# A product moved between its neighbours in units of seven products: two-layer decoder trunk on one Trainium2 core

## The chip, the cores and the metric

The kernel runs on one core of one Trainium2 chip. The metric is the device time of one launch in microseconds (us). Most executions of a kernel agree within 0.3%. The kernel before took 1681.06 us, the median of three runs (1681.12, 1681.06, 1673.86).

## What is computed

The reference is a decoder trunk over 2048 positions of width 1024, in float32: one layer that mixes positions by a short convolution, one layer of attention without softmax, and three norms. Cut to what matters:

```python
h = rmsnorm(x, norm_a)                                   # layer 0
b, c, xin, g = split(h @ w_in, 4)                        # w_in: 1024 x 4096
y = b * causal_conv3(c * xin)
x = x + (y * silu(g)) @ w_out                            # w_out: 1024 x 1024
k, v = split(rmsnorm(x, norm_kv) @ w_kv, 2)              # 8 heads of 64
q, g = split(rmsnorm(x, norm_b) @ w_in_b, 2)             # layer 1
o = stick_breaking_attention(q, k, v)                    # causal, per head
x = x + (o * silu(g)) @ w_out_b
return rmsnorm(x, norm_f)
```

## The kernel before, in words

Activations lie transposed: 128 features on the partitions, positions along the free side, in four chunks of 512 columns (CH=512). Every float32 operand of a matmul is held as a high and a low part in a reduced format, and a product of two operands takes three matmuls (high x high, high x low, low x high) for each 128 rows of the contraction.

**Units of seven products.** The big projections are not done block by block. For two chunks and two blocks of 128 output features, four 128x512 results are made by seven block products in place of eight (the method of Strassen and Winograd). Each product contracts over 512 features: 4 steps (Q=4) of 3 matmuls, so 12 matmuls of 128x512. There are 44 such units: 28 in the first layer's input projection (parts m02 to m07 for chunks 0 and 1, m20 to m27 for chunks 2 and 3; names with B and C), 8 in its output projection (po00 to po03 and po20 to po23; names with o0 to o3, followed by the chunk 0 or 2), and 8 in the projections after it for chunks 0 and 1 (kq0 to kq3, vg0 to vg3).

Three functions make a unit. `fast_operands` (L731) makes seven right operands per pair of chunks (for chunks 0 and 1 of the first projection another function does it, which the change leaves alone), named b11, t1, t2, b22, b21, t3, t4, each in four k-tiles: it loads tiles, takes differences on VectorE (DVE), copies the high part on ScalarE (ACT) and subtracts to get the low part on VectorE, or on GpSimd (POOL) for b21 and t3 of the out units and of the kq and vg units (`late`, L739). `fast_weights` (L771) loads the seven left operands (a11, s1, s2, s4, a12, s3, a22), 512 KB each, through SyncE's queue (SP) in the order of `NAMES`, into a ring of eight tiles. `fast_unit` (L816) issues the products:

- Bank `a` (tag lin, two buffers; traced as fa) is the shared accumulator. It takes a11·b11, s2·t2, s3·t3 and a22·t4 one after the other, and after each of them an engine reads the partial sum: c11 (keep f1), c12 (keep f2), p5, and the last result. The next product into the bank must wait until that read is done.
- Bank `d` (tag z, three buffers; fd) takes s1·t1 (read into p5, keep f5), then s4·b22 (added to c12).
- Bank `e` (tag wt, two buffers; fe) takes a12·b21 alone (added to c11).

In the units of the first projection, and in kq and vg, a keep is a copy by ScalarE. In the out units it is an addition on VectorE of the residual tile (traced as x), which SyncE has loaded from the input; p5 and the sums with d and e are additions on VectorE in every unit.

**The order.** The body isn't emitted as written. A recorder (`Recorder`, L205 to L353) collects all operations of all parts; the table PLAN gives each part a start and an end, an operation's key is its place in its part between them, and `Recorder.order` puts the operations on the engines in turn: the one that can start first by built-in costs, and of equals the one with the lower key. So the order in which a unit is written moves the keys of its operations, and with them operations of all engines in this and in neighbouring parts. Every operation is issued at one line and shows as L353 in the profile; tiles tell them apart. In the trace fa_o is bank a of an out unit, whl_s_o and whl_a_o its left operands, op_t and op_b right operands, xb_kq and op_b_kq the tiles of which the operands of kq and vg are made.

## Time and profile before

| | value |
|---|---|
| profiled execution, own time | 1683.09 us |
| its span, first to last instruction | 1680.9 us |
| median of the three timed runs | 1681.06 us |
| TensorE (PE) busy | 1623.6 us, 97% |
| VectorE (DVE) busy | 1345.1 us, 80% |
| ScalarE (ACT) busy | 787.7 us, 47% |
| GpSimd (POOL) busy | 524.6 us, 31% |
| mean granted TensorE clock | 0.992 |

A row of a timeline gives start, duration, engine, line, operation, output and inputs, tile size, the number of instructions in the row, and in brackets the engine's idle time before it with what ended it. A row of windows gives the stretch, its length, and the busy time of PE, of PE's weight loads (PEld), DVE, ACT and POOL, then the granted TensorE clock, the share of the DMA engines and GB/s. A row of waits gives who waited for whom, the sum in us, how often, and the longest.

On TensorE the last matmuls of the out units of chunks 0 and 1 lie near 726 us of the span, those of chunks 2 and 3 end near 817 us; the kq and vg units follow until about 980 us, with the first of attention among them.

### The profile page before, as it was taken

Reading aid. Unit: us, or ns where it says so; the run is one execution under the profiler, and the core shown is the slowest. Engines: PE = TensorE matmul, PEld = TensorE weight load, DVE = VectorE, ACT = ScalarE, POOL = GpSimd, SP = SyncE. Lnnn points to the kernel's source line nnn. Section 1 sums busy time; section 2 is a strip of 40 time slices with the busy share of each in tenths; the row PEclk is TensorE's granted clock in tenths of the full one; section 3 lists DMA queues with packets and bytes.
Section 4 is the critical chain, followed back from the end, with each engine's and each line's share of the span. In section 5 each row is a group of like instructions: output and inputs, shape, how many; then the busy total and the mean of one; then the engine's idle time right before and its main releaser. Section 6 shows DMA issues by size and latency. Waiting matters only on the chain.

```text
span 1680.9 us, 23871 instructions
## 1 busy us (share of the span) xinstructions
PE 1623.6 (97%) x7828; PEld 1339.8 (80%) x7828; DVE 1345.1 (80%) x1944; ACT 787.7 (47%) x1483; POOL 524.6 (31%) x708
## 2 busy tenths in 40 slices
PE   6999999999999999998999999999999999999896
PEld 5878888888888887877778877887888888888775
DVE  6998788885436349798898788968999988999895
ACT  5444444432213125432544455645556656667452
POOL 5340000000000002357643142333333444556534
PEclk9999999999999999999999999999999999999997
DMA  9458889884473569999677899998756788779744
GB/s 275 163 182 307 296 303 306 278 304 145 147 213 97 192 208 314 365 353 345 213 240 248 288 368 299 357 278 244 222 182 184 229 261 283 247 237 282 228 158 140
DMA packets 226251, 419.48 MB, mean 250 GB/s; under 512 B 21072, under 2 KB 94800, under 8 KB 226128
## 3 DMA queue, kind: packets, MB, share of 16 engines
q1 hardware_dynamic: 194656, 358.15, 63.3%
q10 hardware_dynamic: 31312, 59.79, 12.4%
q8 instruction: 62, 1.02, 0.3%
q14 instruction: 61, 0.50, 0.1%
q0 software_dynamic: 160, 0.02, 0.0%
HBM read 265.06 MB, written 152.83 MB: 249 GB/s over the span
## 4 chain that ended last, share of the span: by engine, by line
PE 75%; DMA 7%; DVE 6%; issue 2%; ACT 2%; POOL 1%; SPq 0%; ACTq 0%; POOLq 0%; DVEq 0%
PE fa_B L353 9%; PE fa_C L353 9%; PE av L353 7%; PE z L353 6%; PE wt L353 6%; PE fd_B L353 5%; PE fd_C L353 4%; PE pob L353 4%; PE fa_o L353 3%; PE fe_C L353 2%; PE fe_B L353 2%; PE pg L353 2%; PE pq L353 2%; PE fa_kq L353 2%; PE pv L353 2%; PE pk L353 2%
## 5 line engine op out<-in xcount | busy, mean ns | idle before, releaser
L353 DVE TENSOR_TENSOR_SCAN R<-R,cy,ones 128x512 f32<-128x512 f32 x192 | 246.3, 1311 | 2.4 <-ACT R L353 2.1
L353 ACT CAST wth<-wt 128x512 fp32r<-128x512 f32 (+2 forms) x320 | 154.4, 526 | 178.9 <-PE wt L353 141.3
L353 DVE TENSOR_TENSOR wtl<-wt,wth 128x512 fp32r<-128x512 f32 (+2 forms) x320 | 180.6, 599 | 37.6 <-ACT wth L353 34.6
L353 PE MATMUL z<-kt,q 128*128 128x512 f32 (+2 forms) x640 | 179.1, 379 | 4.4 <-DMA q<-q_d 2.0
L353 ACT ACTIVATE R<-z 128x512 f32<-128x512 f32 (+2 forms) x320 | 158.9, 545 | 39.8 <-PE z L353 34.5
L353 PE MATMUL wt<-ident,R 128*128 128x128 f32 x1088 | 168.4, 273 | 0.1
L353 POOL COPY halo<-p 128x2 f32<-128x2 f32 x32 | 15.7, 490 | 482.2 <-DVE p L353 482.2
L353 PEld LDWEIGHTS wt<-ident,R 128*128 128x128 f32 x1088 | 133.4, 141 | 21.1 <-DVE R L353 0.7
L353 POOL COPY cy<-R 128x1 f32<-128x1 f32 x192 | 100.5, 526 | 135.8 <-DVE R L353 117.6
L353 PEld LDWEIGHTS z<-kt,q 128*128 128x128 f32 x640 | 111.4, 190 | 23.2 <-ACT R L353 4.5
L353 PE MATMUL av<-wth,vv 128*128 128x512 f32 (+1 forms) x320 | 119.5, 374 | 9.9 <-ACT wth L353 9.1
L353 PE MATMUL av<-wtl,vv 128*128 128x512 f32 (+1 forms) x320 | 122.7, 387 | 0.5 <-DVE wtl L353 0.4
L353 DVE TENSOR_TENSOR_SCAN R<-R,ones 128x256 f32<-128x256 f32 (+3 forms) x128 | 103.8, 838 | 8.8 <-POOL R L353 7.8
L353 POOL TENSOR_SCALAR_AFFINE_SELECT R<-R 128x128 f32<-128x128 f32 x128 | 68.1, 545 | 117.6 <-ACT R L353 116.4
L353 PE MATMUL pob<-og,whl_ob 128*128 128x512 f32 x360 | 102.8, 404 | 0.6 <-DVE x L353 0.4
L353 POOL TENSOR_TENSOR acc_x<-acc_x,sq_x 128x512 f32<-128x512 f32 x52 | 73.8, 1424 | 63.0 <-ACT sq_x L353 61.2
L353 PE MATMUL fa_C<-op_t,whl_s_C 128*128 128x512 f32 x336 | 85.2, 391 | 0.7 <-DVE op_t L353 0.7
L353 PE MATMUL fa_B<-op_t,whl_s_B 128*128 128x512 f32 x336 | 84.9, 390 | 0.0
L353 PEld LDWEIGHTS av<-wth,vv 128*128 128x128 f32 x320 | 60.4, 189 | 26.9 <-ACT wth L353 12.8
L353 PEld LDWEIGHTS fa_C<-op_t,whl_s_C 128*128 128x128 f32 x336 | 62.9, 188 | 14.7 <-DVE op_t L353 1.1
L353 PEld LDWEIGHTS pob<-og,whl_ob 128*128 128x128 f32 x360 | 64.6, 189 | 12.5 <-DVE x L353 0.8
L353 PEld LDWEIGHTS fa_B<-op_t,whl_s_B 128*128 128x128 f32 x336 | 63.0, 188 | 12.9
(581 smaller groups left out, 3779.4 us busy)
## 6 DMA issues: line engine op xcount, KB each, us to landing
kt<-k_d ACTq DMA_DIRECT2D x80, 256.0 KB, 4.6
vv<-v_d ACTq DMA_DIRECT2D x80, 256.0 KB, 4.7
q<-q_d ACTq DMA_DIRECT2D x64, 256.0 KB, 6.3
sw_s_C<-whl_s_C SPq DMA_DIRECT2D x24, 512.0 KB, 3.7
sw_s_B<-whl_s_B SPq DMA_DIRECT2D x24, 512.0 KB, 4.4
whl_s_C<-sw_s_C SPq DMA_DIRECT2D x24, 512.0 KB, 4.3
whl_s_B<-sw_s_B SPq DMA_DIRECT2D x24, 512.0 KB, 4.3
whl_ob<-sw_ob SPq DMA_DIRECT2D x24, 512.0 KB, 5.2
```

Of the source, the lines that this page charges most:

```text
L353: getattr(o.engine.engine, o.name)(*map(real, o.args), **{k: real(v) for k, v in o.kw.items()})
```

## The change

Three edits go together. In `fast_operands` the four t3 operands are made before the loop that loads and makes the four of b21, where the two took turns before. `NAMES` lists s3 ahead of a12, so left operands are loaded in that order. In `fast_unit` s3·t3 and the addition to p5 come right behind s4·b22, and a12·b21 with the addition to c11 comes between s3·t3 and a22·t4. The same seven products are made of the same operands.

```diff
@@ fast_operands
         d = []
         for k in range(Q):
+            operand(key, "t3", k, b[k], late)
+        for k in range(Q):
             d.append(raw("b21", 1, k + Q))
             operand(key, "b21", k, d[k], late)
-            operand(key, "t3", k, b[k], late)
@@
-    NAMES = ("a11", "s1", "s2", "s4", "a12", "s3", "a22")
+    NAMES = ("a11", "s1", "s2", "s4", "s3", "a12", "a22")
@@ fast_unit
         product(d, "s4", "b22", False, True)
         nc.vector.tensor_add(c12, c12, d)
+        product(a, "s3", "t3", False, False)
+        nc.vector.tensor_add(p5, p5, a)
         product(e, "a12", "b21", True, True)
         nc.vector.tensor_add(c11, c11, e)
-        product(a, "s3", "t3", False, False)
-        nc.vector.tensor_add(p5, p5, a)
         product(a, "a22", "t4", False, True)
         return ((c12, p5), (c11, a))
```

What the recorder makes of it is seen in the order of instructions on the engines. From about 1080 us of the trace of before to its end, the order on every engine is the same in both kernels. Three places follow; a row is output, left of the arrow, and inputs, and x3 stands for three matmuls alike.

**TensorE, end of unit o1 of chunk 2.** Before, bank a of o2 (fa_o2_2) follows on the last product of o1, then comes the first product of o3:

```order
L353 MATMUL fa_o1_2_6483<-op0_t4_('o', 2)_3_6686,whl_a22_o1_2_6566 128x512
L353 MATMUL fa_o1_2_6483<-op1_t4_('o', 2)_3_6711,whl_a22_o1_2_6566 128x512
L353 MATMUL fa_o1_2_6483<-op0_t4_('o', 2)_3_6686,whl_a22_o1_2_6566 128x512
L353 MATMUL fa_o2_2_6762<-op_t2_('o', 2)_0_6355,whl_s2_o2_2_6760 128x512 x3
L353 MATMUL fa_o2_2_6762<-op_t2_('o', 2)_1_6384,whl_s2_o2_2_6760 128x512 x3
L353 MATMUL fa_o2_2_6762<-op_t2_('o', 2)_2_6415,whl_s2_o2_2_6760 128x512 x3
L353 MATMUL fa_o2_2_6762<-op_t2_('o', 2)_3_6420,whl_s2_o2_2_6760 128x512 x3
L353 MATMUL fd_o2_2_6782<-op_b22_('o', 2)_0_6241,whl_s4_o2_2_6767 128x512 x3
L353 MATMUL fd_o2_2_6782<-op_b22_('o', 2)_1_6248,whl_s4_o2_2_6767 128x512 x3
L353 MATMUL fd_o2_2_6782<-op_b22_('o', 2)_2_6256,whl_s4_o2_2_6767 128x512 x3
L353 MATMUL fd_o2_2_6782<-op_b22_('o', 2)_3_6263,whl_s4_o2_2_6767 128x512 x3
L353 MATMUL fa_o3_2_6871<-op0_b11_('o', 2)_0_6140,whl_a11_o3_2_6817 128x512
```

After the change, the last product of o1 stands among matmuls of o2's bank d:

```order
L353 MATMUL fd_o2_2_6789<-op_b22_('o', 2)_2_6264,whl_s4_o2_2_6759 128x512
L353 MATMUL fa_o1_2_6515<-op0_t4_('o', 2)_3_6684,whl_a22_o1_2_6569 128x512
L353 MATMUL fd_o2_2_6789<-op_b22_('o', 2)_2_6264,whl_s4_o2_2_6759 128x512
L353 MATMUL fa_o1_2_6515<-op1_t4_('o', 2)_3_6707,whl_a22_o1_2_6569 128x512
L353 MATMUL fd_o2_2_6789<-op_b22_('o', 2)_3_6387,whl_s4_o2_2_6759 128x512 x2
L353 MATMUL fa_o1_2_6515<-op0_t4_('o', 2)_3_6684,whl_a22_o1_2_6569 128x512
L353 MATMUL fd_o2_2_6789<-op_b22_('o', 2)_3_6387,whl_s4_o2_2_6759 128x512
L353 MATMUL fa_o3_2_6869<-op0_b11_('o', 2)_0_6137,whl_a11_o3_2_6786 128x512
L353 MATMUL fa_o3_2_6869<-op1_b11_('o', 2)_0_6230,whl_a11_o3_2_6786 128x512
L353 MATMUL fa_o3_2_6869<-op0_b11_('o', 2)_0_6137,whl_a11_o3_2_6786 128x512
```

The first product of o3 takes the bank that o1 leaves. Its distance from the last matmul into that bank went from 24 matmuls to one.

**TensorE, s3·t3 and a22·t4 of unit o2 of chunk 2.** Before, four matmuls of o3 stand between the two products into bank fa_o2_2:

```order
L353 MATMUL fa_o2_2_6762<-op_t3_('o', 2)_1_6498,whl_s3_o2_2_6833 128x512 x3
L353 MATMUL fa_o2_2_6762<-op_t3_('o', 2)_2_6508,whl_s3_o2_2_6833 128x512 x3
L353 MATMUL fa_o2_2_6762<-op_t3_('o', 2)_3_6518,whl_s3_o2_2_6833 128x512 x3
L353 MATMUL fa_o3_2_6871<-op_t2_('o', 2)_0_6355,whl_s2_o3_2_6908 128x512 x3
L353 MATMUL fa_o3_2_6871<-op_t2_('o', 2)_1_6384,whl_s2_o3_2_6908 128x512
L353 MATMUL fa_o2_2_6762<-op_t4_('o', 2)_0_6603,whl_a22_o2_2_6869 128x512 x3
L353 MATMUL fa_o3_2_6871<-op_t2_('o', 2)_1_6384,whl_s2_o3_2_6908 128x512
L353 MATMUL fa_o2_2_6762<-op_t4_('o', 2)_1_6653,whl_a22_o2_2_6869 128x512 x2
```

And now two matmuls of the moved product (fe_o2_2) and four of o3:

```order
L353 MATMUL fa_o2_2_6753<-op_t3_('o', 2)_0_6482,whl_s3_o2_2_6848 128x512 x3
L353 MATMUL fa_o2_2_6753<-op_t3_('o', 2)_1_6489,whl_s3_o2_2_6848 128x512 x3
L353 MATMUL fa_o2_2_6753<-op_t3_('o', 2)_2_6500,whl_s3_o2_2_6848 128x512 x3
L353 MATMUL fa_o2_2_6753<-op_t3_('o', 2)_3_6509,whl_s3_o2_2_6848 128x512 x3
L353 MATMUL fe_o2_2_6906<-op_b21_('o', 2)_3_6586,whl_a12_o2_2_6856 128x512 x2
L353 MATMUL fa_o3_2_6869<-op_t2_('o', 2)_0_6339,whl_s2_o3_2_6904 128x512 x3
L353 MATMUL fa_o3_2_6869<-op_t2_('o', 2)_1_6360,whl_s2_o3_2_6904 128x512
L353 MATMUL fa_o2_2_6753<-op_t4_('o', 2)_0_6613,whl_a22_o2_2_6861 128x512 x3
L353 MATMUL fa_o3_2_6869<-op_t2_('o', 2)_1_6360,whl_s2_o3_2_6904 128x512
```

Ten of the twelve moved matmuls were put ahead of s3·t3 by the recorder all the same. The distance went from four matmuls to six.

**VectorE, ahead of the second read of bank fa_o2_2 (the addition to x1_2_4).** Before, one of the four differences for the operand t1 of kq (the rows into xb11_kq_0 to xb11_kq_3) stands ahead of that read, one right behind it, and two behind the next addition:

```order
L353 TENSOR_TENSOR op1_b11_kq_1_6892<-xb11_kq_1_6670,op0_b11_kq_1_6881 128x512
L353 TENSOR_TENSOR xb11_kq_0_6606<-xb12_kq_0_6619,xb11_kq_0_6606 128x512
L353 TENSOR_TENSOR x1_3_6_6784<-x1_3_6_6784,fa_o3_2_6871 128x512
L353 TENSOR_TENSOR op1_b11_kq_2_6918<-xb11_kq_2_6677,op0_b11_kq_2_6888 128x512
L353 TENSOR_TENSOR op1_b11_kq_3_6922<-xb11_kq_3_6688,op0_b11_kq_3_6895 128x512
L353 TENSOR_TENSOR x1_3_4_6655<-x1_3_4_6655,fe_o2_2_6899 128x512
L353 TENSOR_TENSOR x1_2_4_6856<-x1_2_4_6856,fa_o2_2_6762 128x512
L353 TENSOR_TENSOR xb11_kq_1_6670<-xb12_kq_1_6625,xb11_kq_1_6670 128x512
L353 TENSOR_TENSOR x1_2_4_6856<-x1_2_4_6856,fd_o2_2_6782 128x512
L353 TENSOR_TENSOR xb11_kq_2_6677<-xb12_kq_2_6633,xb11_kq_2_6677 128x512
L353 TENSOR_TENSOR xb11_kq_3_6688<-xb12_kq_3_6646,xb11_kq_3_6688 128x512
```

And now all four stand ahead of it:

```order
L353 TENSOR_TENSOR op1_b11_kq_0_6895<-xb11_kq_0_6621,op0_b11_kq_0_6877 128x512
L353 TENSOR_TENSOR x1_3_6_6765<-x1_3_6_6765,fa_o3_2_6869 128x512
L353 TENSOR_TENSOR op1_b11_kq_1_6902<-xb11_kq_1_6641,op0_b11_kq_1_6882 128x512
L353 TENSOR_TENSOR op1_b11_kq_2_6910<-xb11_kq_2_6650,op0_b11_kq_2_6888 128x512
L353 TENSOR_TENSOR op1_b11_kq_3_6915<-xb11_kq_3_6666,op0_b11_kq_3_6893 128x512
L353 TENSOR_TENSOR xb11_kq_0_6621<-xb12_kq_0_6673,xb11_kq_0_6621 128x512
L353 TENSOR_TENSOR xb11_kq_1_6641<-xb12_kq_1_6682,xb11_kq_1_6641 128x512
L353 TENSOR_TENSOR xb11_kq_2_6650<-xb12_kq_2_6699,xb11_kq_2_6650 128x512
L353 TENSOR_TENSOR xb11_kq_3_6666<-xb12_kq_3_6712,xb11_kq_3_6666 128x512
L353 TENSOR_TENSOR x1_2_4_6863<-x1_2_4_6863,fa_o2_2_6753 128x512
L353 TENSOR_TENSOR x1_2_4_6863<-x1_2_4_6863,fd_o2_2_6789 128x512
```

Three differences have moved ahead of the read, and the addition of fe_o2_2 to x1_3_4 has moved behind it.

## The prediction

> **What bounds the kernel.** I read the page's table of engines and its chain first, then windows, then TensorE's waits, then the timelines of the two engines that meet in those waits. The page says that TensorE is at work nearly all the time, and that the chain that ended last runs over it:

> ```profile
> span 1680.9 us, 23871 instructions
> PE 1623.6 (97%) x7828; PEld 1339.8 (80%) x7828; DVE 1345.1 (80%) x1944; ACT 787.7 (47%) x1483; POOL 524.6 (31%) x708
> PE 75%; DMA 7%; DVE 6%; issue 2%; ACT 2%; POOL 1%; SPq 0%; ACTq 0%; POOLq 0%; DVEq 0%
> ```

> The change neither adds nor removes a matmul, so it can only move TensorE's idle time, 1680.9 - 1623.6 = 57.3 us in all. Where that lies is seen in windows (columns: stretch, length, then busy time of PE, PEld, DVE, ACT, POOL):

> ```profile
> 120.00:640.00 520.00, 520.00 (x2301) 429.26 (x2301) 341.31 (x538) 179.83 (x305) 25.48 (x58) 1.00 0.70 233
> 640.00:1080.00 440.00, 423.55 (x1960) 342.04 (x1959) 376.78 (x539) 209.25 (x390) 184.84 (x186) 1.00 0.90 307
> 760.00:800.00 40.00, 35.56 (x159) 28.37 (x158) 31.50 (x35) 10.36 (x18) 29.92 (x21) 1.00 0.92 335
> ```

> The first projection with its 28 units fills 120 to 640 us without a gap: 520.00 of 520.00. The out, kq and vg units lie in 640 to 1080, where 440.00 - 423.55 = 16.45 us are idle, 4.4 of them in the 40 us from 760. Behind 1080 us the order on all engines is unchanged. So 16.45 us is the most that can be won; what stands behind can only be moved earlier or later as a whole.

> What the change is about is the next product's wait for the read of the shared bank. TensorE's waits name those readers (us in total, times, longest):

> ```profile
> PE fa_o L353 <- DVE x L353: 5.9, 4, 2.3
> PE fa_kq L353 <- DVE f_kq L353: 0.6, 1, 0.6
> PE fa_vg L353 <- DVE f_vg L353: 0.4, 1, 0.4
> ```

> No row of this view has a wait of fa_B or fa_C for a reader: in the first projection the reads are covered already. The rest is in the timeline of TensorE, around units o1, o2 and o3 of chunk 2, and kq0 and vg3:

> ```profile
> 765.84 0.84 PE L353 MATMUL fa_o<-op_t_('o', 2)_3_6518,whl_s_o 128*128 128x512 f32 x3
> 767.58 0.73 PE L353 MATMUL fa_o<-op_t_('o', 2)_0_6603,whl_a_o 128*128 128x512 f32 x2 [0.90 <-DVE x L353]
> ...
> 786.75 0.39 PE L353 MATMUL fd_o<-op_t_('o', 2)_0_6272,whl_s_o 128*128 128x512 f32 x1
> ...
> 789.25 0.39 PE L353 MATMUL fd_o<-op_t_('o', 2)_3_6347,whl_s_o 128*128 128x512 f32 x1
> 790.85 0.97 PE L353 MATMUL fa_o<-op_t_('o', 2)_0_6464,whl_s_o 128*128 128x512 f32 x3 [1.22 <-DVE x L353]
> ...
> 793.73 0.84 PE L353 MATMUL fa_o<-op_t_('o', 2)_0_6355,whl_s_o 128*128 128x512 f32 x3
> 794.41 0.39 PE L353 MATMUL fa_o<-op_t_('o', 2)_1_6384,whl_s_o 128*128 128x512 f32 x1
> 797.12 0.96 PE L353 MATMUL fa_o<-op_t_('o', 2)_0_6603,whl_a_o 128*128 128x512 f32 x3 [2.33 <-DVE x L353]
> 814.37 0.96 PE L353 MATMUL fa_o<-op_t_('o', 2)_0_6603,whl_a_o 128*128 128x512 f32 x3 [1.50 <-DVE x L353]
> 852.65 3.77 PE L353 MATMUL fa_kq<-op_t_kq,whl_a_kq 128*128 128x512 f32 x14 [0.64 <-DVE f_kq L353]
> 976.11 0.49 PE L353 MATMUL fa_vg<-op_t_kq,whl_a_vg 128*128 128x512 f32 x1 [0.42 <-DVE f_vg L353]
> ```

> Five of these waits stand between s3·t3 and a22·t4, the place that gets twelve matmuls as cover by the code: 0.90 + 2.33 + 1.50 + 0.64 + 0.42 = 5.79 us. The sixth, 1.22 us at 790.85, is at s3·t3 of o2, which the change brings closer to its reader. From 786.75 to 789.25 are eleven starts: 2.50 / 11 = 0.227 us per matmul, so twelve cover 2.72 us.

> **The change, part by part.**

> *First projection, 28 units: 0.* With no gap there is nothing to win. The loss is bounded by the cover: between s2·t2 and s3·t3 stood 24 matmuls and stand 12 now, 2.72 us, for this copy:

> ```profile
> L353 ACT COPY f_B<-fa_B 128x512 f32<-128x512 f32 x28 | 16.4, 586 | 24.5 <-PE fa_B L353 24.0
> ```

> A read without cover costs what o1 shows. Its last s3 matmul started at 765.84 + 2 x 0.227 = 766.29, the next into that bank at 767.58: 1.29 us, or 1.06 beyond the pitch, with an addition of 0.67 us in between. A copy of 0.59 fits into 2.72 even behind one more of its kind. I take 0; if ScalarE came over 1.5 us late in every unit, each such us would cost 28 us, but its busy share of 47% speaks against that.

> *t3 made ahead of b21, on GpSimd: 0.* The recorder had already put them so in the second half, as GpSimd's timeline of before shows (t3 is op_t, b21 is op_b):

> ```profile
> 738.33 1.28 POOL L353 TENSOR_TENSOR op_t_('o', 2)_0_6464<-xb_('o', 2)_0_5598,op_t_('o', 2)_0_6464 128x512 fp32r<-128x512 f32 x1 [9.81 <-ACT op_t_('o', 2)_0_6464 L353]
> 745.47 1.28 POOL L353 TENSOR_TENSOR op_t_('o', 2)_3_6518<-xb_('o', 2)_3_5879,op_t_('o', 2)_3_6518 128x512 fp32r<-128x512 f32 x1
> 747.71 1.28 POOL L353 TENSOR_TENSOR op_b_('o', 2)_0_6549<-xb_('o', 2)_4_6466,op_b_('o', 2)_0_6549 128x512 fp32r<-128x512 f32 x1
> ```

> In the out units of chunk 0 and in kq, b21's first part falls behind at most two more such subtractions, 2 x 1.28 = 2.6 us, and its product is wanted 12 matmuls or 2.72 us later than before. The bounds are 0 and 2.6 us in each of two places; I take 0, since the later use covers it.

> *o1 of chunk 2: -0.07.* Its a22·t4 now has the twelve matmuls of o2's first product ahead of it, so 0.90 goes. But that product is what used to stand ahead of o3, whose first matmul needs the bank that o1 leaves and has one matmul of cover where it had 24: 1.06 - 0.23 = +0.83.

> *o2 of chunk 2: +0.9.* Here VectorE sets the time. Its timeline, with the read of 790.85's wait at 790.12 and that of 797.12's at 796.39:

> ```profile
> 785.77 1.52 DVE L353 TENSOR_TENSOR xb_kq<-xb_kq,xb_kq 128x512 f32<-128x512 f32 x1
> 789.52 0.68 DVE L353 TENSOR_TENSOR x<-x,fe_o 128x512 f32<-128x512 f32 x1
> 790.12 0.67 DVE L353 TENSOR_TENSOR x<-x,fa_o 128x512 f32<-128x512 f32 x1
> 790.72 0.68 DVE L353 TENSOR_TENSOR xb_kq<-xb_kq,xb_kq 128x512 f32<-128x512 f32 x1
> 791.92 2.88 DVE L353 TENSOR_TENSOR xb_kq<-xb_kq,xb_kq 128x512 f32<-128x512 f32 x2
> 794.72 1.75 DVE L353 TENSOR_TENSOR whl_s_kq<-fr_a_kq,whl_s_kq 128x512 fp32r<-128x512 f32 x1
> 796.39 0.67 DVE L353 TENSOR_TENSOR x<-x,fa_o 128x512 f32<-128x512 f32 x1
> ```

> In the new order three differences for kq, 0.68 + 2.88 = 3.56 us by these rows, stand ahead of the first read, and the addition from fe (0.60 to the next start) goes behind it: 3.56 - 0.60 = 2.96 us later. The read starts at 793.1 and s3·t3 at 793.8. Those twelve matmuls took 2.88 us (790.85 to 793.73), so they end near 796.7; then come the six now standing ahead of a22·t4, 6 x 0.227 = 1.36, and a22·t4 starts at 798.0 where it started at 797.12, with the same work behind it. Its own wait has gone (796.4, the start of the last s3 matmul, plus 1.29 is 797.7). So 2.33 us are won and some 3.2 lost. The bounds of the three differences are 3 x 0.68 and 3 x 1.75 by the rows 790.72 and 794.72, less 0.60: 1.4 to 4.65 us, which puts this term between -0.6 and +2.6. I stay with the rows' own sum.

> [...]

> *o3 of chunk 2: -1.50.* a22·t4 gets twelve matmuls ahead where it had none; 2.72 covers 1.06 and one VectorE operation of 1.75 ahead of the reader, nearly.

> The distances that follow are counted in the order of instructions. *o3 of chunk 0: +0.6.* Cover shrinks from five matmuls to two: 1.06 - 2 x 0.227. *kq0: -0.64*, cover from 5 to 25. *kq2: +0.4*, whose first matmul waits for a bank with three matmuls of cover where it had nine: 1.06 - 3 x 0.227. *kq1, vg:* nothing; vg3 keeps seven matmuls and its 0.42.

> *Attention's start, 980 to 1080 us: 0.* Its first operations change places by a few rows; the idle time there is part of the 16.45 us and could grow or shrink by some us, for which no row speaks.

> *Left operands.* One load of 512 KB (s1 of o3) is issued later, 21 matmuls or 4.8 us ahead of its use, and lands in:

> ```profile
> whl_s_o<-sw_s_o SPq DMA_DIRECT2D x16, 512.0 KB, 6.8
> ```

> That would be 6.8 - 4.8 = 2.0 us late, but o2's s3·t3 waits for VectorE at that time; I take 0 and keep +2.0 as the other end.

> **The sum.** 0 + 0 - 0.07 + 0.9 - 1.50 + 0.6 - 0.64 + 0.4 + 0 = -0.3 us. The profiled execution took 1683.09 us, so 1682.8; it was 2.03 us above the median of the runs (1681.06), so the forecast against that is **1680.7 us**: no difference. Half a per cent, 8.4 us, is about what a measurement of this kernel can tell from no change.

> **Rivals.**

> *All five waits go, nothing new.* If VectorE keeps its old pace at o2 and the banks come free in time, 5.79 us are won: 1675.3. For it speaks that each reader gets cover by the code; against it, that the recorder took ten of the twelve moved matmuls of o2 back ahead of s3·t3. With all other gaps of 640 to 1080 us it would be 16.45: 1664.6, for which nothing speaks.

> *The recorder undoes it.* It fills gaps by its own costs whatever the writing, and waits move but do not go: 1681.1.

> *VectorE's differences end ahead of the readers, on the slower side.* In o2, o3 and kq0 both reads of the bank stand among differences for kq. If three of them stand ahead of a read, each at 1.75 us as at 794.72, the read is 4.65 us late. In o2 that makes the term +2.6 in place of +0.9; at four more reads, each with 2.72 us of cover, it costs 4.65 - 2.72 = 1.9 each. Sum: -0.3 + 1.7 + 7.7 = +9.1 us, 1690.2. It decides from the point where over 2.72 us of VectorE's work stands between a bank's last matmul and its reader. For it: DVE is busy 31.50 of 40.00 us there and GpSimd 29.92. Against it: of the five waits of before only o2's, 2.33 us, is longer than a read at once would give (1.06) by as much as an operation of VectorE; o3's 1.50 is by a third of one. [...]

> **How the numbers follow.** My sum 0.44, the recorder's undoing 0.12, all waits gone 0.16, the slow rival 0.21, more than any of these on the fast side (gaps at the start of attention, up to 16.45 us) 0.07. Of the slow rival's chance a small part stays within half a per cent, and so does nearly all of the third case. That gives faster by over 0.5% 0.10, within 0.67, slower 0.23. The range leaves out the extremes: low 1672, between 1675.3 and 1664.6; high 1691, above the slow rival.

> **What would show it.** Right: windows of 120 to 640 us still full; no wait of about 2.33 us ahead of o2's a22·t4, but one of some 4 us ahead of its s3·t3; a new wait near 0.8 us at o3's first product; none of 1.50 ahead of its a22·t4; 640 to 1080 us again with 15 to 18 us idle. Wrong: gaps of fa_B or fa_C on ScalarE's copies, which my zero for 28 units excludes; waits of over 2 us for weight loads; or a changed idle sum behind 1080 us, where I count on the old one.

## The result and the profile after

The changed kernel took **1692.87 us** (median of 7 runs, 1687.89 to 1695.05) beside 1679.93 us for the kernel before (7 runs, 1673.86 to 1683.46). The ratio is 1.008, with a 95% interval of 1.0059 to 1.0102: slower by 12.9 us. The forecast was 1680.7 with a range up to 1691, so the time lies above the range.

The page of the changed kernel, first its span, then busy time by engine, then the chain that ended last by engine:

```profile
span 1686.1 us, 23866 instructions
PE 1627.3 (97%) x7828; PEld 1341.5 (80%) x7828; DVE 1334.5 (79%) x1944; ACT 788.6 (47%) x1483; POOL 530.2 (31%) x708
PE 74%; DVE 7%; DMA 6%; issue 3%; ACT 2%; POOL 1%; ACTq 0%; SPq 0%; POOLq 0%; DVEq 0%
```

Its profiled execution took 1687.89 us, the lowest of its seven runs, while the profiled execution of before (1683.09) lies above six of the seven runs of its kernel. The two spans differ by only 5.2 us for that reason, and a reader who compared these two pages alone would put the loss at a third of a per cent. A second profile of each kernel, unchanged, has 1673.3 us of span for before and 1689.4 for after, a difference of 16.1.

The same windows as before the change, for the kernel after (stretch, length, busy PE, PEld, DVE, ACT, POOL, granted TensorE clock, DMA share, GB/s), with three stretches in which the clock is below 1.00:

```profile
120.00:640.00 520.00, 518.39 (x2296) 428.15 (x2295) 332.41 (x535) 179.31 (x304) 26.84 (x58) 1.00 0.70 232
640.00:1080.00 440.00, 420.69 (x1914) 339.44 (x1912) 364.13 (x528) 203.22 (x378) 191.85 (x184) 0.98 0.87 298
...
720.00:760.00 40.00, 35.69 (x153) 28.78 (x152) 28.95 (x59) 13.72 (x24) 16.53 (x12) 0.91 0.87 305
800.00:840.00 40.00, 36.35 (x146) 28.04 (x147) 32.91 (x45) 18.09 (x33) 21.28 (x14) 0.96 0.66 216
840.00:880.00 40.00, 36.30 (x154) 28.68 (x153) 34.98 (x45) 19.37 (x35) 24.50 (x17) 0.96 0.64 202
```

The stretch of 720 to 760 us in the kernel before:

```profile
720.00:760.00 40.00, 38.20 (x169) 29.63 (x168) 38.45 (x62) 15.24 (x27) 23.55 (x18) 1.00 1.00 347
```

The reader is to see two things. From 720 to 760 us TensorE is idle for 4.31 us in place of 1.80, and in that stretch its mean clock is 0.91 in place of 1.00, which is another 3.4 us: the engine counts as busy while its matmuls start 0.42 us apart at a clock of 0.50, as the rows below show, in place of 0.227. And VectorE, 38.45 us busy there before, is 28.95 us busy now.

Idle time of TensorE and time lost to the half clock, after less before, in us. The lost time is the sum of (1 - clock) over windows of half a us, so 6.8 us at half clock lose 3.4:

| stretch | first pair: idle, clock | second pair: idle, clock |
|---|---|---|
| 40 to 640 | +1.6, 0 | +1.1, 0 |
| 640 to 720 | +1.3, 0 | +1.5, 0 |
| 720 to 760 | +2.5, +3.4 | +2.5, +3.4 |
| 760 to 800 | -1.4, 0 | +0.2, 0 |
| 800 to 840 | +2.1, +1.7 | +0.5, +1.7 |
| 840 to 880 | +1.0, +1.7 | +1.1, +3.4 |
| 880 to 1080 | -2.7, 0 | -2.7, 0 |
| 40 to 1080 | **+11.3** | **+12.7** |
| 1080 to 1640 | -2.8, -5.1 | +3.2, +1.7 |

Up to 1080 us the two pairs agree with each other and with the median. Behind 1080, where the order of instructions is the same in both kernels, they go apart. One wait for ScalarE makes most of that. From the timeline of TensorE, first profile of before, then second profile of after:

```profile
1566.12 0.80 PE L353 MATMUL av<-wth,vv 128*128 128x512 f32 x1 [5.21 <-ACT wth L353]
```

```profile
1575.46 0.50 PE L353 MATMUL av<-wth,vv 128*128 128x512 f32 x1 [4.00 <-ACT wth L353]
```

The second profile of before doesn't wait at that matmul, the first of after waits 0.42 us, and over all 15 profiles the wait lies anywhere between 0 and 5.21. So this wait and the time lost to the half clock behind it (3.41 us in the first row) are chance of one execution, and neither gain nor loss of the change.

**The largest single place is unit o0 of chunk 2**, of which the prediction has no term. TensorE around s2·t2 and s3·t3 of that unit, kernel before:

```profile
734.83 0.84 PE L353 MATMUL fa_o<-op_t_('o', 2)_3_6420,whl_s_o 128*128 128x512 f32 x3
...
738.99 0.47 PE L353 MATMUL fa_o<-op_t_('o', 2)_0_6464,whl_s_o 128*128 128x512 f32 x1 [1.28 <-ACT sq_x L353]
```

The same place in the kernel after:

```profile
737.87 0.84 PE L353 MATMUL fa_o<-op_t_('o', 2)_3_6413,whl_s_o 128*128 128x512 f32 x3
...
741.86 0.62 PE L353 MATMUL prb_x<-ident,r 128*128 128x128 f32 x4 [0.43 <-DVE t_x L353]
746.03 0.77 PE L353 MATMUL fa_o<-op_t_('o', 2)_0_6482,whl_s_o 128*128 128x512 f32 x1 [3.55 <-issue]
746.60 0.63 PE L353 MATMUL fa_o<-op_b_('o', 2)_0_6137,whl_a_o 128*128 128x512 f32 x1
747.02 0.63 PE L353 MATMUL fa_o<-op_b_('o', 2)_0_6230,whl_a_o 128*128 128x512 f32 x1
```

From the start of the last three s2·t2 matmuls to s3·t3 it was 738.99 - 734.83 = 4.16 us, and is 746.03 - 737.87 = 8.16. The wait of 3.55 us is put down to "issue", that is, to nothing that the profile could name; what ends at that moment is found on VectorE. VectorE before, the read of bank a into x1_2_0 being the row at 738.21:

```profile
736.87 0.68 DVE L353 TENSOR_TENSOR xb_('o', 2)_0_5598<-xb_('o', 2)_4_6089,xb_('o', 2)_0_5598 128x512 f32<-128x512 f32 x1
...
738.21 0.67 DVE L353 TENSOR_TENSOR x<-x,fa_o 128x512 f32<-128x512 f32 x1
...
740.99 0.69 DVE L353 TENSOR_TENSOR xb_('o', 2)_1_5793<-xb_('o', 2)_5_6096,xb_('o', 2)_1_5793 128x512 f32<-128x512 f32 x1
```

VectorE after, the same read being the last row:

```profile
740.21 0.69 DVE L353 TENSOR_TENSOR xb_('o', 2)_0_5766<-xb_('o', 2)_4_6112,xb_('o', 2)_0_5766 128x512 f32<-128x512 f32 x1
...
740.95 0.69 DVE L353 TENSOR_TENSOR xb_('o', 2)_1_5844<-xb_('o', 2)_5_6147,xb_('o', 2)_1_5844 128x512 f32<-128x512 f32 x1
...
741.70 0.69 DVE L353 TENSOR_TENSOR xb_('o', 2)_2_5853<-xb_('o', 2)_6_6186,xb_('o', 2)_2_5853 128x512 f32<-128x512 f32 x1
742.30 1.25 DVE L353 SCALAR_TENSOR_TENSOR t_x<-t_x,v_x 128x4 f32<-128x4 f32 x1
743.48 0.68 DVE L353 TENSOR_TENSOR xb_('o', 2)_3_5875<-xb_('o', 2)_7_6310,xb_('o', 2)_3_5875 128x512 f32<-128x512 f32 x1
744.08 1.26 DVE L353 SCALAR_TENSOR_TENSOR r<-t_x,r 128x4 f32<-128x4 f32 x1
745.26 0.68 DVE L353 TENSOR_TENSOR x<-x,fa_o 128x512 f32<-128x512 f32 x1
```

The rows xb_('o', 2)_0 to _3 are the differences of which t3 is made. Before, one of the four stood ahead of the read and three behind it. Now all four stand ahead of it, with pieces of two small chains for the norm (t_x, r) in between. Counted from the last s2·t2 row the read starts after 745.26 - 737.87 = 7.39 us; before it was 738.21 - 734.83 = 3.38. It ends at 745.94, and s3·t3 starts 0.09 us later. The three places listed ahead of the prediction do not include this one.

Then TensorE runs at half clock. Windows of the kernel after:

```profile
743.00:745.00 2.00, 0.00 (x0) 0.00 (x0) 2.00 (x3) 1.20 (x3) 2.00 (x2) 1.00 1.02 385
745.00:747.00 2.00, 0.97 (x2) 0.83 (x3) 1.90 (x4) 0.18 (x1) 2.00 (x3) 0.59 0.76 238
747.00:749.00 2.00, 2.00 (x6) 1.59 (x5) 1.12 (x3) 0.45 (x1) 0.77 (x1) 0.50 0.74 230
749.00:751.00 2.00, 2.00 (x6) 1.52 (x6) 0.00 (x0) 0.00 (x0) 0.00 (x0) 0.50 0.89 281
751.00:753.00 2.00, 2.00 (x8) 1.59 (x7) 0.00 (x0) 0.00 (x0) 0.00 (x0) 0.71 0.05 14
```

The pitch of matmuls agrees with the clock column: 747.02 - 746.60 = 0.42 us between starts, where the rows in the prediction gave 0.227. Six instructions of PE stand in 2 us. VectorE, at 0.00, waits for their product until 754.21 us, and ScalarE and GpSimd wait behind it.

### The profile page after: what moved, and what is told of

Same layout as the page of the kernel before. It is cut to its first block, busy times and chain, and to the rows that moved or that the text cites. A ratio compares the mean times of both kernels' runs of the same rounds, so it can differ in the third digit from the quotient of the medians.

```text
span 1686.1 us, 23866 instructions
## 1 busy us (share of the span) xinstructions
PE 1627.3 (97%) x7828; PEld 1341.5 (80%) x7828; DVE 1334.5 (79%) x1944; ACT 788.6 (47%) x1483; POOL 530.2 (31%) x708
## 4 chain that ended last, share of the span: by engine, by line
PE 74%; DVE 7%; DMA 6%; issue 3%; ACT 2%; POOL 1%; ACTq 0%; SPq 0%; POOLq 0%; DVEq 0%
PE fa_B L353 9%; PE fa_C L353 8%; PE av L353 7%; PE z L353 6%; PE wt L353 6%; PE pob L353 5%; PE fd_B L353 4%; PE fd_C L353 4%; PE fa_o L353 3%; PE fa_vg L353 3%; PE pv L353 2%; PE fe_B L353 2%; PE pq L353 2%; PE fe_C L353 2%; PE fa_kq L353 2%
## 5 line engine op out<-in xcount | busy, mean ns | idle before, releaser
L353 DVE TENSOR_TENSOR_SCAN R<-R,cy,ones 128x512 f32<-128x512 f32 x192 | 247.9, 1323 | 2.7 <-ACT R L353 2.6
L353 ACT CAST wth<-wt 128x512 fp32r<-128x512 f32 (+3 forms) x320 | 154.5, 526 | 169.2 <-PE wt L353 137.1
L353 DVE TENSOR_TENSOR wtl<-wt,wth 128x512 fp32r<-128x512 f32 (+3 forms) x320 | 180.2, 599 | 30.4 <-ACT wth L353 27.2
L353 PE MATMUL z<-kt,q 128*128 128x512 f32 (+2 forms) x640 | 179.6, 377 | 3.8 <-DMA kt<-k_d 1.4
L353 ACT ACTIVATE R<-z 128x512 f32<-128x512 f32 (+2 forms) x320 | 159.3, 546 | 40.7 <-PE z L353 32.9
L353 PE MATMUL wt<-ident,R 128*128 128x128 f32 x1088 | 166.5, 272 | 1.0 <-DVE wtl L353 1.0
L353 POOL COPY halo<-p 128x2 f32<-128x2 f32 x32 | 15.7, 491 | 472.6 <-DVE p L353 437.9
L353 PEld LDWEIGHTS wt<-ident,R 128*128 128x128 f32 x1088 | 132.6, 140 | 21.0 <-DVE wtl L353 1.6
L353 POOL COPY cy<-R 128x1 f32<-128x1 f32 x192 | 102.1, 535 | 144.0 <-DVE R L353 127.7
L353 PEld LDWEIGHTS z<-kt,q 128*128 128x128 f32 x640 | 111.6, 188 | 23.5 <-ACT R L353 5.2
L353 PE MATMUL av<-wtl,vv 128*128 128x512 f32 (+1 forms) x320 | 122.6, 387 | 1.6 <-DVE wtl L353 1.5
L353 PE MATMUL av<-wth,vv 128*128 128x512 f32 (+1 forms) x320 | 118.2, 370 | 2.8 <-ACT wth L353 2.8
L353 DVE TENSOR_TENSOR_SCAN R<-R,ones 128x256 f32<-128x256 f32 (+3 forms) x128 | 101.8, 828 | 2.3 <-POOL R L353 1.6
L353 PE MATMUL pob<-og,whl_ob 128*128 128x512 f32 x360 | 102.7, 403 | 0.6 <-DVE x L353 0.4
L353 POOL TENSOR_SCALAR_AFFINE_SELECT R<-R 128x128 f32<-128x128 f32 x128 | 67.6, 541 | 101.0 <-ACT R L353 100.1
L353 POOL TENSOR_TENSOR acc_x<-acc_x,sq_x 128x512 f32<-128x512 f32 x52 | 75.7, 1459 | 73.9 <-ACT sq_x L353 61.1
L353 PE MATMUL fa_C<-op_t,whl_s_C 128*128 128x512 f32 x336 | 86.2, 390 | 0.7 <-DVE op_t L353 0.7
L353 PE MATMUL fa_B<-op_t,whl_s_B 128*128 128x512 f32 x336 | 84.7, 389 | 0.0
L353 PEld LDWEIGHTS av<-wth,vv 128*128 128x128 f32 x320 | 60.1, 188 | 18.2 <-ACT wth L353 6.6
L353 PEld LDWEIGHTS pob<-og,whl_ob 128*128 128x128 f32 x360 | 64.5, 188 | 12.6 <-DVE x L353 0.9
L353 PEld LDWEIGHTS av<-wtl,vv 128*128 128x128 f32 x320 | 60.2, 188 | 18.0 <-DVE wtl L353 5.5
L353 PEld LDWEIGHTS fa_C<-op_t,whl_s_C 128*128 128x128 f32 x336 | 62.8, 188 | 14.6 <-DVE op_t L353 1.1
## 6 DMA issues: line engine op xcount, KB each, us to landing
sw_s_C<-whl_s_C SPq DMA_DIRECT2D x24, 512.0 KB, 4.0
sw_s_B<-whl_s_B SPq DMA_DIRECT2D x24, 512.0 KB, 4.2
whl_s_C<-sw_s_C SPq DMA_DIRECT2D x24, 512.0 KB, 4.3
whl_s_B<-sw_s_B SPq DMA_DIRECT2D x24, 512.0 KB, 4.2
whl_ob<-sw_ob SPq DMA_DIRECT2D x24, 512.0 KB, 5.0
```

The source lines that it names most:

```text
L353: getattr(o.engine.engine, o.name)(*map(real, o.args), **{k: real(v) for k, v in o.kw.items()})
```

## The experiments

**Theory A:** VectorE's reads of the shared bank now stand behind operand work that the new writing order put ahead of them, at o0 and at o2, and each such wait costs itself and half clock behind it. **Its rivals:** moving the product is itself what costs, wherever the reads stand; one of the other two edits (t3 ahead of b21, the order of left operands) costs it alone; or the loss is spread over left operands that land late. The last three kernels ask what a wait costs by way of the clock.

The experiments that move single operations do so in the recorder's finished list: `ahead(x, y)` puts the operation x right ahead of y, an operation being named by engine, output and input; `put(group, place)` does so for several.

### The reads put back: e1_read_o0 and e2_reads

The first is the kernel after, with only the read of o0 ahead of the four differences. The second moves the read into x1_2_4 of unit o2 as well.

```diff
 ops = nc.order(PLAN)
+ahead((DVE, "x1_2_0", "fa_o0_2"), (DVE, "xb12_('o', 2)_0", "xb22_('o', 2)_4"))
```

> The changed kernel, with one VectorE addition (the second read of bank a of unit o0 of chunk 2, into x1_2_0) put ahead of the four differences for t3 instead of behind them; nothing else moves. Theory A (the reads of the shared bank stand behind operand differences in VectorE's queue, and a gap of over about 2.5 us also halves TensorE's clock for 3.4 or 6.8 us): the wait of 3.55 us ahead of s3 x t3 of o0 shrinks under 1.5, the clock stays at 1.00 from 740 to 760 us, and the time falls by about 6 us, to some 1687. Rival B (the loss is spread over left operands that land late and over the first projection): that wait may go, but the time stays at 1690 to 1694.

```diff
+ahead((DVE, "x1_2_4", "fa_o2_2"), (DVE, "xb11_kq_0", "xb12_kq_0"))
```

> As the run before, and also the same read of unit o2 of chunk 2 (into x1_2_4) put ahead of the four differences for kq. Theory A: the wait of 2.48 us ahead of s3 x t3 of o2 goes too, with its 3.4 us at half clock; some 4 us less again, about 1683. Rival B: 1690 to 1694.

e1_read_o0 took 1684.26 us (10 runs, 1680.07 to 1694.4), 1.0025 of before (1.0001 to 1.0049). Taken by the two ratios, 1.008 - 1.0025 = 0.0055, one moved operation gives back some 9 of the 13 us, give or take 5 by the two intervals. TensorE at o0 in e1_read_o0:

```profile
735.26 0.84 PE L353 MATMUL fa_o<-op_t_('o', 2)_3_6413,whl_s_o 128*128 128x512 f32 x3
...
739.85 0.62 PE L353 MATMUL prb_x<-ident,r 128*128 128x128 f32 x4 [1.03 <-DVE t_x L353]
740.23 0.48 PE L353 MATMUL fa_o<-op_t_('o', 2)_0_6483,whl_s_o 128*128 128x512 f32 x1
```

VectorE at that place:

```profile
737.60 0.68 DVE L353 TENSOR_TENSOR x<-x,fa_o 128x512 f32<-128x512 f32 x1
738.20 0.68 DVE L353 TENSOR_TENSOR xb_('o', 2)_0_5766<-xb_('o', 2)_4_6112,xb_('o', 2)_0_5766 128x512 f32<-128x512 f32 x1
```

From s2·t2 to s3·t3 it is 740.23 - 735.26 = 4.97 us where it was 8.16, and the clock is full from 740 to 756: 3.2 + 3.4 = 6.6 us at this place. Some of it goes to smaller waits that follow at once (0.44 us for an operand from GpSimd at 741.61): the next s2·t2 starts 749.89 - 735.26 = 14.63 us behind this one, where it was 757.41 - 737.87 = 19.54, so 4.9 us are left. The "issue" of the profile was VectorE's read.

e2_reads took 1685.0 us (10 runs, 1679.12 to 1689.09), 1.0027 (1.0006 to 1.0047): no further gain. The wait at o2's s3·t3, 2.45 us in e1_read_o0, is gone, but 0.59 and 0.56 us for other reads come at 802 and 803 us, and the waits for operands of kq stay. The half of theory A that blames o2's read falls. A reading that fits, and that no run isolates, is that VectorE has the same work to do there in any order, so that one of its readers or users waits. The profiled executions of e1_read_o0 and e2_reads lie 4 and 6 us under the medians of their runs, so their waits show the fast end.

### The edits apart: u_unit_names and u_ops

The first has the moved product and the new order of left operands, and makes t3 and b21 by turns as before. The second has only t3 ahead of b21.

```diff
# u_unit_names: before, with
-    NAMES = ("a11", "s1", "s2", "s4", "a12", "s3", "a22")
+    NAMES = ("a11", "s1", "s2", "s4", "s3", "a12", "a22")
...
+        product(a, "s3", "t3", False, False)
+        nc.vector.tensor_add(p5, p5, a)
         product(e, "a12", "b21", True, True)
         nc.vector.tensor_add(c11, c11, e)
-        product(a, "s3", "t3", False, False)
-        nc.vector.tensor_add(p5, p5, a)
```

> The kernel before with two of the three edits: the product moved in the unit, and the order of loads; t3 and b21 take turns as before. By the order, the read into x1_2_0 then stands behind one difference for t3, as before the change. Theory A: no wait over 2 us ahead of s3 x t3 of o0; within 4 us of the kernel before, 1678 to 1684. If the moved product itself costs (theory C): 1688 or more.

```diff
# u_ops: before, with
         for k in range(Q):
+            operand(key, "t3", k, b[k], late)
+        for k in range(Q):
             d.append(raw("b21", 1, k + Q))
             operand(key, "b21", k, d[k], late)
-            operand(key, "t3", k, b[k], late)
```

> The kernel before with the first edit alone: t3 made ahead of b21. By the order, the read into x1_2_0 then stands behind all four differences for t3. Theory A: a wait ahead of s3 x t3 of o0 and a halved clock behind it, 5 us or more over the kernel before, 1685 to 1690. Theory C (the moved product costs): within 2 us of the kernel before.

u_unit_names took 1685.93 us (10 runs, 1681.28 to 1691.3), 1.0034 (1.0016 to 1.0052), above the 1678 to 1684 of theory A and below the 1688 of its rival. Its profiled execution is the fastest of the ten. At o0 it waits 0.46 us, but a22·t4 of o3 waits 3.27 us for VectorE (816.74 us). u_ops took 1679.61 us (10 runs, 1675.74 to 1685.48), 0.999 (0.9969 to 1.001): no change, where theory A had 1685 to 1690. Its profiled execution was the slowest of the ten, and has 1.43 and 3.85 us of waits for an operand of o0 with half clock behind them. The read of o0 stands behind all four differences there too, but it waits for its own product, whose last operand came late:

```profile
746.27 0.69 DVE L353 TENSOR_TENSOR x<-x,fa_o 128x512 f32<-128x512 f32 x1 [2.45 <-PE fa_o L353]
```

So t3 ahead of b21 alone is not the cause, and neither part holds the read of o0 up as their combination does: 5.7 us and about nothing apart, 12.9 together. It is the recorder that put both together in this way.

No run has the new order of left operands alone. TensorE's waits for left operands from 100 to 1080 us sum to 0 and 0.3 us in the two profiles of before, to 2.0 and 2.3 in those of after, and to 1.0 in e1_read_o0. u_ops, with the old order, has 2.2. So late left operands are some 2 us of the loss, and they come with the recorder's order as much as with the list in `NAMES`.

### The two kernels again, and before with the late read: b_again, a_again, e3_late_read

Second profiles of both kernels, unchanged, and the kernel before with the other three differences put ahead of the read of o0.

> The kernel before, word for word, for a second profile. If the wait of 5.21 us near 1566 us and the two stretches at half clock (1137 and 1564 us) of its first profile are the luck of that execution, they are not all there, and the span is 3 to 8 us shorter. If they belong to the kernel, the span is 1680 to 1682 again.

> The changed kernel, word for word, for a second profile. Expected by theory A: again a wait of over 3 us ahead of s3 x t3 of o0 of chunk 2 with 3.4 us lost to a halved clock behind it; the waits near 802 and 867 us again, their half clock perhaps not, since it seems to fall by stretches of about 3.4 us and needs luck at gaps near 2.5.

```diff
 ops = nc.order(PLAN)                          # e3_late_read: before, with
+for k in (1, 2, 3):
+    ahead((DVE, "xb12_('o', 2)_%d" % k, "xb22_('o', 2)_%d" % (k + 4)), (DVE, "x1_2_0", "fa_o0_2"))
```

> The kernel before, with three differences for t3 (into xb12_1 to xb12_3) put ahead of the second read of bank a of unit o0 of chunk 2 on VectorE, as they stand after the change; all else as before. Theory A: the wait there grows from 1.3 to 3 us or more, the clock halves behind it, and the time rises by 4 to 7 us, to about 1685. Theory B or C (the place does not matter): within 2 us of 1680.

The second profiles are read in the table above. At o0 the second profile of after repeats the first: a wait of 3.55 us, 8.16 us from s2·t2 to s3·t3, and 3.4 us lost to the clock. e3_late_read took 1681.08 us (10 runs, 1677.71 to 1687.55), 1.0019 (0.9999 to 1.0038), so some 3 us, not surely more than nothing, and below the 4 to 7 of theory A. TensorE at o0:

```profile
739.61 1.73 PE L353 MATMUL fa_o<-op_t_('o', 2)_0_6464,whl_s_o 128*128 128x512 f32 x3 [3.08 <-issue]
```

VectorE's read there:

```profile
738.83 0.67 DVE L353 TENSOR_TENSOR x<-x,fa_o 128x512 f32<-128x512 f32 x1
```

The wait grew by 1.8 us, from 1.28 to 3.08, and 5.12 us were lost to the half clock behind it in this profile; the wait is again given as "issue" and ends 0.11 us behind the read. Later waits shrink a little (o2's s3·t3 waits 0.68 in place of 1.22), but most of the 6.9 us stays in this profile: beside the second profile of before, TensorE is 0.2 us late at the s2·t2 of o0, 5.3 us late at o3's a22·t4 (818.32 and 813.03 us) and still 4.2 us late at 1000 us. The ten runs show less, some 3 us. The place is a cause, and its price is not the same in every kernel and execution.

### The idea by itself: p_move, p_both and b_hoist

p_move is the kernel before in the recorder's order, with nothing moved but the twelve matmuls of a12·b21 in o1, o2 and o3 of chunk 2, and what has to follow them: on VectorE an addition of that product and two operations for left operands of kq change places. p_both also puts three reads at the place in VectorE's order where their product ends. b_hoist moves three reads alone; two of them fell into the middle of their product, so p5 of o2 and o3 lacks half of s3·t3 there.

```diff
 ops = nc.order(PLAN)                          # p_move: before, with
+for u in (1, 2, 3):
+    put(<a12·b21 of o{u}, chunk 2>, <behind the last matmul of its s3·t3>)
```

> The kernel before, its order kept as it is, and only the product a12 x b21 of o1, o2 and o3 of chunk 2 moved by hand between s3 x t3 and a22 x t4 on TensorE (with it the additions that read it). This is the idea of the change without the recorder's reshuffle. If cover for the third read is what was wanting: the waits 0.90, 2.33 and 1.50 us go and nothing comes, about 1676 (4.7 us under the kernel before). If VectorE's queue sets the time of the reads (theory A): the waits ahead of a22 x t4 go, but s3 x t3 of o2 and o3, now twelve matmuls earlier, wait by as much for the second read; within 2 us of the kernel before.

```diff
+for out, bank, product in (("x1_2_4", "fa_o2_2", "t2"), ("x1_2_5", "fa_o2_2", "t3"), ("x1_2_7", "fa_o3_2", "t3")):
+    put(<the read of bank into out>, <behind the last matmul of product>)
```

> As the run before, and on VectorE the reads of bank a into x1_2_4, x1_2_5 (o2) and x1_2_7 (o3) put where their product ends, ahead of the differences and subtractions that stood there. Theory A: cover and queue together take away the waits of o1, o2 and o3, 5.9 us, less what the operands of kq are late: 2 to 5 us under the kernel before. If VectorE's work as a whole is the bound from 780 to 860 us: the waits turn up at kq0, and the time is that of the kernel before within 2 us.

```diff
 ops = nc.order(PLAN)                          # b_hoist: before, with
+ahead((DVE, "x1_2_4", "fa_o2_2"), (DVE, "xb11_kq_0", "xb12_kq_0"))
+ahead((DVE, "x1_2_5", "fa_o2_2"), (DVE, "xb11_kq_3", "xb12_kq_3"))
+ahead((DVE, "x1_2_7", "fa_o3_2"), (DVE, "whl_s4_kq0", "fr_a12_kq0"))
```

> The kernel before, with three reads of the shared bank put ahead of other work on VectorE: of o2 into x1_2_4 ahead of the first difference for kq, of o2 into x1_2_5 ahead of the last one, of o3 into x1_2_7 ahead of a subtraction for a left operand. If those reads set the time there, waits of 1.22, 2.33 and 1.50 us shrink by some 3 us together, about 1677. If VectorE's work as a whole sets it from 780 to 860 us (as the run with both reads moved suggests), the waits turn up a little later and the time stays within 1.5 us of 1680.

| kernel | us (lowest to highest, runs) | ratio to before |
|---|---|---|
| p_move | 1683.29 (1676.51 to 1687.76, 10) | 1.0028 (1.0007 to 1.0049) |
| p_both | 1685.61 (1682.47 to 1686.33, 7) | 1.0053 (1.0035 to 1.0071) |
| b_hoist | 1682.37 (1675.3 to 1685.58, 10) | 1.0022 (1.0001 to 1.0043) |

The move on its own doesn't pay, and by their medians all three lie above both of the times that had been expected for them. p_move's profiled execution is the fastest of the ten: o2's a22·t4 waits 0.47 us in place of 2.33, but o1's 1.38 in place of 0.90 and o3's 2.92 in place of 1.50, and an operand of the moved product comes 0.79 us late. By its ratio the move itself costs some 5 us (0.0028 x 1676; 1 to 8 by the interval), so this rival holds for a part; where the whole change is made, one read of o0 is the larger part. In b_hoist the waits of 1.22 and 2.33 us at o2 became one of 3.27, and in p_both a read at the head of VectorE's queue had to wait for its residual tile, so that o3's first product waited 6.06 us:

```profile
788.89 1.29 DVE L353 TENSOR_TENSOR x<-x,fa_o 128x512 f32<-128x512 f32 x2 [9.22 <-DMA x<-in_xT_dram]
```

So p_both doesn't tell what the reads are worth where that tile is there in time.

### What a wait costs: f_fill, g_small, g_large

f_fill keeps the order of after and puts 15 more runs of the first matmul of o1's a11·b11 ahead of o0's s3·t3, where TensorE waited; in the kernel that matmul begins the sum of its bank (start=True), so these are meant as work without effect. In g_small and g_large ScalarE makes its copy of the partial sum 8 times in 12 units, or 11 times in 6 units, of the first projection, so that TensorE waits there.

```diff
 ops = nc.order(PLAN)                          # f_fill: after, with
+first = <first matmul of a11·b11, o1, chunk 2>
+k = <place of the first matmul of s3·t3, o0, chunk 2>
+ops[k:k] = [first] * 15
```

> The changed kernel with fifteen matmuls more, which keep TensorE at work through the wait of 3.55 us ahead of s3 x t3 of o0: copies of the first matmul of o1 into its own bank, which each start that bank anew, so the result is untouched. Useful work starts no earlier than before. If half of the loss there is the clock (theory A): no half clock from 740 to 756 us, and 3.4 us less than the changed kernel, about 1689. If the halved clock only shows the idle time and costs nothing of its own: 1692 to 1693.

```diff
 ops = nc.order(PLAN)                          # g_small: after, with
+for unit in C1 to C6 and B1 to B6, chunk 2:   # g_large: C1 to C6, * 10
+    k = <place of ScalarE's copy f2 of the unit>
+    ops[k:k] = [ops[k]] * 7
```

> The changed kernel with TensorE made to wait a little in twelve units of the first projection (C1 to C6 and B1 to B6 of chunk 2): ScalarE makes the copy of the second read of bank a eight times in place of once, so s3 x t3 waits some 1.5 us. Twelve waits, 18 us idle. If only long gaps halve the clock, no stretch below full clock comes with them.

> The same with six units (C1 to C6) and eleven copies, so six waits of about 3.0 us, 18 us idle again. If gaps of this size halve the clock for 3.4 or 6.8 us, most of the six are followed by such a stretch, and 10 to 20 us more are lost than with twelve small waits; if the clock does not depend on the gap, the two take the same time.

f_fill took 1690.86 us (5 runs, 1689.1 to 1693.67), 1.0076 (1.0051 to 1.01). TensorE at o0:

```profile
740.33 3.69 PE L353 MATMUL fa_o<-op_b_('o', 2)_0_6137,whl_a_o 128*128 128x512 f32 x15
744.17 0.47 PE L353 MATMUL fa_o<-op_t_('o', 2)_0_6482,whl_s_o 128*128 128x512 f32 x1 [0.15 <-issue]
```

Its windows behind that:

```profile
745.00:750.00 5.00, 5.00 (x24) 4.13 (x23) 1.83 (x4) 0.58 (x1) 0.94 (x1) 1.00 0.66 214
```

With the wait filled, the clock stays full. But VectorE still has its gap, 1.83 us busy of 5.00, since the products that it reads come as late as before. The work is 3.1 us earlier than in the second profile of after until 797 us; then o2's s3·t3 waits 3.14 us in place of 2.12, and at 841 us 0.8 us are left. So in these profiles the 3.4 us lost to the half clock at o0 are for the most part hidden by what follows, and **what e1_read_o0 recovers there would be above all the late start of s3·t3**, which holds up both engines. By the medians this is not settled: f_fill and the kernel after overlap widely, and in e3_late_read the lost time stayed.

g_small took 1728.25 us (2 runs), 1.0315 (1.0264 to 1.0366), and g_large 1718.5 (2 runs), 1.0257 (1.0198 to 1.0315). The waits came out at 2.29 and 4.13 us, larger than I had sized them (1.5 and 3.0), so whether small waits leave the clock alone could not be told from these. TensorE in g_small, twelve matmuls behind the wait in a row:

```profile
472.12 4.61 PE L353 MATMUL fa_C<-op_t,whl_s_C 128*128 128x512 f32 x12 [2.29 <-ACT f_C L353]
...
541.85 3.01 PE L353 MATMUL fa_B<-op_t,whl_s_B 128*128 128x512 f32 x12 [2.29 <-ACT f_B L353]
```

The same wait is followed by twelve matmuls in 4.61 us at one place and in 3.01 at another. In windows of 2 us just behind, the clock is 0.56 and 1.00:

```profile
472.00:474.00 2.00, 1.88 (x5) 1.50 (x6) 0.69 (x1) 0.07 (x1) 0.00 (x0) 0.56 0.31 125
543.00:545.00 2.00, 2.00 (x11) 1.65 (x10) 1.97 (x5) 0.10 (x1) 0.00 (x0) 1.00 0.28 76
```

From 400 to 660 us, six of the eight waits of 2.29 us in g_small were followed by half clock, and all four waits of 4.13 us in g_large.

## Why the prediction was wrong

Point by point, by its own steps:

- **The step that failed: "t3 made ahead of b21, on GpSimd: 0".** It asked only when GpSimd makes b21 and when b21 is wanted. But for t3 VectorE first takes four differences, and these moved ahead of a read of the shared bank on VectorE's own queue. With it fell the sum, which **had no term for o0 of chunk 2**: s3·t3 there starts 4.0 us later (8.16 less 4.16) and 3.4 us are lost to the half clock behind it. e1_read_o0 shows the step: one read put ahead of the four differences takes back some 9 of the 13 us.
- **A wait was priced at its own length.** The clock term was missing altogether. How much of it reaches the end depends on what is late next: at o0 of the kernel after little of it did (f_fill), at o0 of the kernel before most of it stayed (e3_late_read).
- *First projection, 0:* nearly. None of its units waits for ScalarE's copies. The loss in both profiles of after is one left operand that comes 1.05 us late, at 351.54 us in the first.
- *o1, -0.07:* held. The wait of 0.90 is gone, and o3's first product waits 0.69 and 0.70 in the two profiles, where +0.83 was forecast. Not in the sum are two waits close by, 0.50 us for an operand (767.90) and 0.61 for a read of bank d (769.95).
- *o2, +0.9:* the mechanism held and the size was off. The 2.33 is gone and s3·t3 waits instead, 2.48 and 2.12 us, not 4. The three rows below are TensorE after, at o3's first product, o2's s3·t3 and kq:

```profile
790.67 0.50 PE L353 MATMUL fa_o<-op_b_('o', 2)_0_6137,whl_a_o 128*128 128x512 f32 x1 [0.69 <-DVE x L353]
...
802.40 0.96 PE L353 MATMUL fa_o<-op_t_('o', 2)_0_6482,whl_s_o 128*128 128x512 f32 x3 [2.48 <-DVE x L353]
...
867.11 1.20 PE L353 MATMUL fa_kq<-op_t_kq,whl_a_kq 128*128 128x512 f32 x4 [1.70 <-DVE op_t_kq L353]
```

  VectorE after, ahead of that read, has the four differences at 0.83 us each on average:

```profile
798.42 3.33 DVE L353 TENSOR_TENSOR xb_kq<-xb_kq,xb_kq 128x512 f32<-128x512 f32 x4
801.67 0.68 DVE L353 TENSOR_TENSOR x<-x,fa_o 128x512 f32<-128x512 f32 x1
```

- *o3, -1.50:* held; its a22·t4 has no wait in the kernel after.
- *o3 of chunk 0, +0.6:* 0.33 us at 728 us. *kq0, -0.64, and kq2, +0.4:* a wait for a read in kq remains, 0.57; the larger waits there are for operands, 1.17 and 0.86 us before and 1.70 and 1.09 now, with half clock behind them in both profiles of after (and in the second of before).
- *Left operands, 0 with an end at +2.0:* a12, now behind s3 in the queue, lands late for o2's moved product, 0.95 and 1.29 us.
- *Attention's start, 0:* the idle time from 880 to 1080 us fell by 2.7 us in both pairs; it could go either way, by the text, and went the good way.
- *Behind 1080 us nothing:* the order is the same. The waits there differ between two executions of one kernel by more than 5 us, so the profiles can't decide it; the medians fit with nothing.

**The slow rival had the mechanism.** It said that VectorE's differences would end ahead of the readers and that this decides where over 2.72 us of VectorE's work stands between a product and its read. At o0 it was over 5 us (740.21 to 745.26). The rival put the place at o2, o3 and kq0, with 1.7 us more at o2 and 1.9 at each of four more reads; that its price of 1690.2 us is nearest to the measured time is luck, as it comes from other terms than those that cost the time. Its 1.75 us for a difference does occur: of the 96 differences for right operands in the first profiles of the two kernels, the 55 that no row of GpSimd overlaps took 0.68 to 0.70 us, the other 41 took 0.68 to 1.79. But the four ahead of o2's read took 3.33 us together.

What e1_read_o0 leaves, some 4 us over before, is about what the moved product costs by itself (p_move), and in its profile it is spread over waits of 0.2 to 2.5 us from 640 to 880 us; e2_reads and p_move show that mending one of them makes another. Which of them make up the 4 us stays open. None of the versions beats the kernel before clear of the noise.

## What to carry to other kernels

When a change of writing order goes through a scheduler, list for each read of a shared bank what now stands ahead of it in its own engine's queue, in every unit and not only where there was a wait before; cover on TensorE says nothing about that. Price a wait by what the engines behind it then lack, and look at the clock column beside it: from 749 to 751 us of the kernel after TensorE was busy for 2.00 of 2.00 us, at a clock of 0.50. And compare medians first, then two profiles of each kernel, since one profile here carried a chance wait of 5 us and hid 8 of the 13.

## What the runs showed of the hardware

**Tiny VectorE operations beside GpSimd took up to 1.28 us.** Rows of SCALAR_TENSOR_TENSOR on 128x4, such as t_x and r, took 0.13 to 0.17 us where no row of GpSimd overlaps them (59 in the first profile of before, 60 in the first of after). The two at 742.30 and 744.08 above, where GpSimd subtracts for t3, took 1.25 and 1.26; the longest, of 1.28, is in the kernel before, at 739.60. GpSimd in the kernel after:

```profile
741.68 1.85 POOL L353 TENSOR_TENSOR op_t_('o', 2)_0_6482<-xb_('o', 2)_0_5766,op_t_('o', 2)_0_6482 128x512 fp32r<-128x512 f32 x1 [6.69 <-ACT op_t_('o', 2)_0_6482 L353]
743.49 1.82 POOL L353 TENSOR_TENSOR op_t_('o', 2)_1_6489<-xb_('o', 2)_1_5844,op_t_('o', 2)_1_6489 128x512 fp32r<-128x512 f32 x1
```

These end at 743.53 and 745.31 us, and the two tiny operations 0.02 and 0.03 us behind them (743.55 and 745.34). Beyond the usual 0.16 us the two took some 2.2 of the 4.0 us by which the read of o0 is late. That GpSimd is what holds them up is read from these times; no run takes its subtractions away from there.
